# Three heads' keys and queries asked for before the top-k search, in free slots instead of a four-tile ring

## The chip, the cores and the metric

The kernel runs on one core of one Trainium2 chip. A time is device microseconds (us) from the start to the end of one execution. Before the change it is 2321.21 us, the median of three runs (2320.97 to 2325.77). The profile comes from one further execution, which took 2315.68 us.

## The reference

One layer of a decoder block on x of shape 1 x 1024 x 1024: half a SwiGLU feed-forward, a mixer of three branches, half a SwiGLU feed-forward. The mixer, cut to what matters here:

```python
h = rms_norm(x, mix_pre_g)
c_q, c_kv, k_idx_raw, w_idx_raw, u_glu, q_mem, gate_logits = jnp.split(h @ w_in, cuts, axis=-1)
y_a = dsa_attention(...) @ w_dsa_o    # 8 heads of 64; each row attends to its top 256 keys
y_b = conv_module(...)                # causal convolution of 31 taps, ends in w_conv_out
y_m = memory_attention(...) @ w_mem_o # 4 heads of 128 over 256 memory rows
merged = g_a * y_a + g_b * y_b + g_m * y_m      # g_*: sigmoid of the gate logits
return x + rms_norm(merged @ w_out, mix_post_g)

# in dsa_attention, for a block of 128 rows:
score = where(causal, sum over index heads of w * relu(q_idx . k_idx), -1e30)
_, sel = lax.top_k(score, 256)
s = q_lat . ckv[sel]                  # the same number as q . k of the head
p = softmax(where(sel <= position, s, -1e30))
o = (p @ ckv[sel]) @ w_uv             # the same number as p @ v of the head
```

## The kernel before

Everything is kept transposed, in blocks of 128 partitions, and a float32 product is made of three products of a high and a low part (`mm3`, lines 144 to 146). The program runs through feed-forward 1 (to about 700 us), the projections of the mixer, the top-k search with the gate projections beside it (to about 1270 us), the attention with the output projections of the branches as filler (to about 1520 us), the rest of the mixer, and feed-forward 2.

SBUF is 50 equal slots. `blk` takes the slot that has been free longest, `free` gives one back. A ring (`ring(qk=4)`, `rt("qk", ...)`) is a set of slots used in turn: with four tiles it holds K and Q of two heads, and the load of head h + 2 into the tiles of head h has to wait until head h's scores have been computed. The queries, keys and values of all heads lie in DRAM (`qk_spill`, `v_spill`), written by the projections.

`attn` (line 803) goes over two column halves, c = 0 and c = 1 (512 query rows each), and over 8 heads in each, so 16 head steps, which are called h0 to h15 here. A step loads K (256 KB in c = 0, 512 KB in c = 1) and Q (one load of 256 KB and two of 128 KB), four loads in all, issued on GpSimd (POOL), whose loads form the software queue q0. Then come two groups of two row blocks: `weights_of` (line 838) computes the scores (PE, line 851), masks and softmaxes them on VectorE (DVE) and ScalarE (ACT), and `weigh` (line 865) transposes the weights of the group before (line 893), splits them, and multiplies by V (line 881). V is loaded on SyncE (SP), 512 KB a tile, for four heads at a time, by `load_v` (line 781); these loads and all other SP ones are in the hardware queue q1. While a group waits for its softmax, `mix` takes pieces of the generator `outputs` (line 1103): the conv branch through `w_conv_out`, the memory branch through `w_mem_o` with its eight `om` tiles (line 1110), and the first half of the DSA branch. `branch` reads the gates back from `gate_spill` as `sigr` (line 925).

The order of each engine's instructions is not the program's order. A scheduler lays them out once, when the kernel is built, with its own picture of when an operand is there, and the engine then goes through them strictly in turn, and each one waits on its semaphores. A load on POOL that waits for a slot therefore holds up every load behind it on POOL.

In the names of the rows, `K` and `Q` are the tiles of a head, `cbh`/`cbl` the conv branch's parts, `woh`/`wol` those of an output weight, `wor` the raw weight, `st` the staging of the gates.

Of the kernel before, what the change touches and what calls it, by code (L numbers as in the profile page):

```python
# [8 lines left out]
F32 = mybir.dt.float32  # L9
F32R = mybir.dt.float32r  # L10
# [8 lines left out]
P = 128  # L19
# [12 lines left out]
H_A, DH = 8, 64  # L32
# [12 lines left out]
class Kern:  # L45
# [637 lines left out]
    def mem_attn(self):  # L683
        nc, S = self.nc, self.S
        K = self.weight("mk", self.mkv[0].rearrange("p (a b) -> p a b", a=4), [P, 4, NMEM], None, "wr2")
        V = self.weight("mv", self.mkv[1].rearrange("p (a b) -> p a b", a=2), [P, 2, 512], None, "wr2")
# [4 lines left out]
        def scores(h, c):  # L691
# [7 lines left out]
            for t2 in range(2):  # L699
                ps = self.bank("ms").rearrange("p (a b) -> p a b", a=2)  # L700
                for e in range(2):
                    ts = slice((2 * t2 + e) * P, (2 * t2 + e + 1) * P)
                    self.mm3(ps[:, e], (q[:, 0, ts], q[:, 1, ts]), (K[0][:, h], K[1][:, h]), True, True)
                es = slice(2 * t2, 2 * t2 + 2)
# [44 lines left out]
        self.drop("mq", "pm", "pT", "st2")  # L749
        self.free(K, V)  # L750

# [51 lines left out]
    def attn(self):  # L803


        nc, S = self.nc, self.S
        O = S["O"]
        prev = V = None
        self.filled = None
        for c in range(2):  # L810
            if c:
                self.banks(s=[(0, 1)], tp=[2, 3, 4], po=[5], fl=[6, 7])
            for h in range(H_A):
                e = h % 2
                if e == 0:
                    O.append(self.blk("O", [P, 2, 512], F32R))
                K = self.rt("qk", "K", [P, (4 * c + 4) * P], F32R)
                Q = self.rt("qk", "Q", [P, 2, 512], F32R)
                self.load_stack(K, 4 + h // 2, e, 0, (4 * c + 4) * P)
                self.load_stack(Q[:, 0], h // 2, e, c * 512, c * 512 + 512)  # L820
                for r in range(2):
                    nc.gpsimd.dma_start(Q[r * 64:r * 64 + 64, 1].bitcast(F32),
                                      self.qk[h // 2, 1 - r, e * 64:e * 64 + 64, c * 512:c * 512 + 512])
                for g in range(2):
                    i0 = 4 * c + 2 * g
                    p, qk = self.weights_of(Q, K, i0)
                    yield (0.2 * i0 + 0.3) * FILL_A[i0 // 4]
                    if prev:
                        yield from self.weigh(*prev, qk)
                    if h % 4 == 0 and g == 0:  # L830
                        if V:
                            self.free(V)
                        V = self.load_v(h // 4, c)
                    prev = (h, g, i0, p, V, O[-1])
        yield from self.weigh(*prev, None)
        self.free(V)

    def weights_of(self, Q, K, i0):

        nc = self.nc  # L840
        sc = DH ** -0.5
        pair = []
        for i in (i0, i0 + 1):
            n = (i + 1) * P
            ng = 1 if n <= 512 else 2
            n2 = n // ng
            ps = self.bank("s")
            ps = (ps[:, None] if len(ps.shape) == 2 else ps)[:, :ng, :n2]
            for a in range(ng):
                for z in range(2):  # L850
                    mm = nc.tensor.matmul(ps[:, a], Q[:, z, i % 4 * P:(i % 4 + 1) * P], K[:, a * n2:(a + 1) * n2],  # L851
                                          start=z == 0, stop=z == 1)
            p = self.rt("p", "p", [P, n])
            mx = self.sm("amx", 1)
            nc.vector.tensor_tensor_reduce(out=p.rearrange("p (a b) -> p a b", a=ng), in0=ps,
                                           in1=self.S["mask"][i].rearrange("p (a b) -> p a b", a=ng), scale=-sc, scalar=3e38,
                                           op0=OP.add, op1=OP.min, accum_out=mx)
            sm = self.sm("asm", 1)
            nc.scalar.activation(p, p, AF.Exp, bias=mx, scale=-1.0, accum_out=sm)
            nc.vector.reciprocal(sm, sm)  # L860
            nc.vector.tensor_scalar_mul(p, p, sm)
            pair.append(p)
        return pair, mm
# [109 lines left out]
    def build(self):  # L973
        nc, A, S = self.nc, self.A, self.S
# [8 lines left out]
        X, kept, g = {}, [], None  # L983
        for t in range(NT):
            x = self.rt("xt", "x", [P, D])
            nc.sync.dma_start(x, A["x"][t * P:(t + 1) * P])
            if t == 0:
                g = self.bcast("gpre", A["ffn1_pre_g"])
# [85 lines left out]
        for _ in fill:  # L1074
            pass
        self.masks()
        self.topk()
        self.drop("acc", first=True)
        acc = [self.conv(m, u[m]) for m in range(4)]
        self.banks(cn=[0, 1, 2, 3], fl=[4, 5, 6, 7])  # L1080
        cn = self.conv_norm(acc)
        self.ring(qk=4)
        next(cn)
        for e in ends[:-2]:
            self.run(e)
# [31 lines left out]
        self.mix(self.attn(), fill, 1.0)  # L1117
        for _ in fill:
            pass
        self.drop("qk", "p", "pT", "wr", "st", "w")  # L1120
        self.ring(wr=3, w=6, st=3)
        self.free(S["packs"])
        self.banks(two=[(0, 1), (2, 3)], tp=[4, 5, 6, 7], one=[4, 5, 6, 7])
# [6 lines left out]
        g = self.bcast("gpre", A["ffn2_pre_g"])  # L1130
# [5 lines left out]
        for t in range(NT):  # L1136
            c, s = t // 4, slice((t % 4) * P, (t % 4 + 1) * P)
# [348 lines left out]
```

## Time and profile before

| | us |
|---|---|
| median of three runs | 2321.21 |
| lowest, highest | 2320.97, 2325.77 |
| the profiled execution | 2315.68 |
| its span (first to last instruction) | 2313.9 |
| PE busy, of the span | 2226.9 |
| DVE busy, of the span | 1713.8 |

So 1.8 us of the profiled execution lie around its span, and it took 5.53 us less than the median. PE, the matrix engine, is busy 96% of the span; what it is not busy is the waiting of PE, and most of that stands in a few gaps. In the rows below an entry of the timeline is: start in us, duration in us, engine, line, operation, output<-input, the shape, how many such instructions the row takes together, and in brackets the idle time of the engine just before it with what ended it. The granted clock of PE is given as a share of 2.4 GHz: 0.50 is its lower level of 1.2 GHz.

### The profile page before, as it was taken

The numbers are of one execution on the slowest core, as the hardware profiler recorded it, in microseconds if no ns is written. First come the engines' busy times: TensorE is split into PE (matmuls) and PEld (weight loads), VectorE is DVE, ScalarE is ACT, GpSimd is POOL, SyncE is SP. The second block draws the span as 40 slices with busy tenths as digits, with TensorE's granted clock in tenths as the row PEclk, the third lists the DMA queues.
The fourth block names the chain that finished last, engine by engine and source line by source line (L and its number), as shares of the span: only waits on it lengthen the run. The fifth ranks groups of instructions, "written<-read, shape, count | busy, mean of one in ns | idle before, by whom it ended". The sixth has DMA issues, their size and how long they took to land.

```text
span 2313.9 us, 29081 instructions
## 1 busy us (share of the span) xinstructions
PE 2226.9 (96%) x10800; PEld 1370.7 (59%) x10800; DVE 1713.8 (74%) x3000; ACT 1167.5 (50%) x1971; POOL 370.9 (16%) x326
## 2 busy tenths in 40 slices
PE   8799999999999999999999789999899999999998
PEld 5344444444447987888887677778644444444443
DVE  7787777766577699997559677885777777777657
ACT  6644444444435343598995445453564444444423
POOL 2221111111100000120000213330321111111200
PEclk9799999999999999999999999999999999999999
DMA  8111111111224105334332656442422111111112
GB/s 291 44 57 56 59 59 55 55 55 55 86 70 156 51 28 199 129 128 128 101 101 88 187 152 171 132 164 109 146 73 68 57 58 56 55 56 55 45 56 91
DMA packets 163828, 218.87 MB, mean 95 GB/s; under 512 B 26053, under 2 KB 122821, under 8 KB 163687
## 3 DMA queue, kind: packets, MB, share of 16 engines
q1 hardware_dynamic: 141158, 202.23, 26.8%
q0 software_dynamic: 22528, 14.80, 2.6%
q8 instruction: 84, 1.38, 0.2%
q14 instruction: 58, 0.47, 0.1%
HBM read 171.79 MB, written 45.09 MB: 94 GB/s over the span
## 4 chain that ended last, share of the span: by engine, by line
PE 69%; issue 14%; DVE 9%; DMA 3%; ACT 3%; POOL 1%; SPq 0%; POOLq 0%; ACTq 0%; DVEq 0%
PE banks L144 22%; PE banks L146 22%; PE banks L145 21%; PE banks L881 1%; PE banks L851 1%; DVE acc L611 1%; DMA Q<-qk_spill 1%; DMA K<-qk_spill 1%; PE banks L893 1%; DVE xl L283 1%; DVE wts L262 1%; ACT junka L170 1%; DMA qk_spill<-qst 1%; ACT junka L245 1%; PE banks L424 1%
## 5 line engine op out<-in xcount | busy, mean ns | idle before, releaser
L146 PE MATMUL banks<-wds,h 128*128 128x512 f16 x704 | 266.8, 379 | 2.5 <-DVE h L262 2.5
L144 PE MATMUL banks<-xh,wts 128*128 128x512 f16 x704 | 267.7, 380 | 0.9 <-ACT xh L282 0.8
L146 PE MATMUL banks<-xh,wts 128*128 128x512 f16 x704 | 267.3, 380 | 0.0
L145 PE MATMUL banks<-xl,wts 128*128 128x512 f16 x704 | 267.3, 380 | 0.0
L145 PE MATMUL banks<-wds,h 128*128 128x512 f16 x704 | 266.8, 379 | 0.0
L144 PE MATMUL banks<-wds,h 128*128 128x512 f16 x704 | 266.7, 379 | 0.0
L1363 DVE SCALAR_TENSOR_TENSOR y<-banks,scal,y 128x512 f32<-128x512 f32 x288 | 209.4, 748 | 76.0 <-PE banks L146 65.6
L144 PE MATMUL banks<-xh,wh 128*128 128x512 f32 x576 | 226.2, 393 | 0.0
L146 PE MATMUL banks<-xh,wl 128*128 128x512 f32 x576 | 225.9, 393 | 0.0
L145 PE MATMUL banks<-xl,wh 128*128 128x512 f32 x576 | 225.5, 391 | 0.0
L144 PE MATMUL banks<-xh,wt 128*128 128x512 f16 x528 | 202.5, 384 | 4.6 <-DVE t L214 2.8
L146 PE MATMUL banks<-xh,wt 128*128 128x512 f16 x528 | 202.3, 383 | 0.4 <-DVE wt L262 0.4
L145 PE MATMUL banks<-xl,wt 128*128 128x512 f16 x528 | 202.5, 384 | 0.0
L261 ACT ACTIVATE wds<-wd,scal 128x1024 f16<-128x1024 f32 x44 | 47.9, 1139 | 252.7 <-DVE scal L230 230.1
L611 DVE SCALAR_TENSOR_TENSOR acc<-u,convc,acc 128x1023 f32<-128x1023 f32 (+14 forms) x120 | 151.7, 1264 | 0.9
L1311 ACT ACTIVATE sil<-sil,scal 128x512 f32<-128x512 f32 x88 | 63.2, 718 | 142.3 <-DVE sil L1310 142.3
L471 ACT ACTIVATE junka<-sc,tk_neg,tk_sg 128x512 bf16<-128x512 f32 (+1 forms) x124 | 124.1, 1001 | 12.4 <-DVE tk_cand L489 9.4
L1216 POOL TENSOR_TENSOR ws<-wg 128x512 f32<-128x512 f32 x22 | 44.0, 2002 | 499.3 <-DVE wds L262 381.1
L245 ACT ACTIVATE junka<-sil 128x1024 bf16<-128x1024 f32 x44 | 46.5, 1057 | 150.7 <-DVE sil L1327 150.7
L146 PEld LDWEIGHTS banks<-xh,wl 128*128 128x128 f32 x576 | 108.4, 188 | 22.3 <-DVE wl L130 0.2
L145 PEld LDWEIGHTS banks<-xl,wh 128*128 128x128 f32 x576 | 108.4, 188 | 21.5
L144 PEld LDWEIGHTS banks<-xh,wh 128*128 128x128 f32 x576 | 108.4, 188 | 21.3 <-ACT xh L129 0.3
(366 smaller groups left out, 4830.9 us busy)
## 6 DMA issues: line engine op xcount, KB each, us to landing
wg<-in_ffn_w_gu SPq DMA_DIRECT2D x44, 512.0 KB, 3.5
wu<-in_ffn_w_gu SPq DMA_DIRECT2D x44, 512.0 KB, 3.6
wd<-in_ffn_w_down SPq DMA_DIRECT2D x44, 512.0 KB, 4.1
wr<-in_w_in SPq DMA_DIRECT2D x38, 512.0 KB, 3.6
gate_spill<-st SPq DMA_DIRECT2D x24, 512.0 KB, 2.7
x_spill<-xres SPq DMA_DIRECT2D x16, 512.0 KB, 2.6
qk_spill<-qst SPq DMA_DIRECT2D x32, 256.0 KB, 3.3
sigr<-gate_spill SPq DMA_DIRECT2D x16, 512.0 KB, 6.2
```

What stands on the lines that cost most here:

```text
L144: self.first = mm(out, a[0], b[0], start=start, stop=False)
L145: mm(out, a[0], b[1], start=False, stop=False)
L146: return mm(out, a[1], b[0], start=False, stop=stop)
L170: self.nc.scalar.activation(self.junk(x.shape), x, AF.Square, accum_out=ss)
L245: self.nc.scalar.activation(self.junk(x.shape), x, AF.Square, accum_out=ss)
L261: self.nc.scalar.activation(hi, raw, AF.Copy, scale=s)
L262: self.nc.vector.scalar_tensor_tensor(lo, raw, s, hi, op0=OP.mult, op1=OP.subtract)
L471: nc.scalar.activation(self.junk((P, ns[q])), sc[q], AF.Sign, bias=bias[:, z:z + 1], scale=scale, accum_out=cnt[:, z:z + 1])
L611: nc.vector.scalar_tensor_tensor(a[:, s:], u[:, :T - s], self.cc[:, m, j:j + 1], a[:, s:], op0=OP.mult, op1=OP.add)
L1216: V.tensor_add(a[:, 0], lo[:, :, P:], hi[:, :, P:])
L1311: nc.scalar.activation(o, o, AF.Silu, scale=iv)
L1363: V.scalar_tensor_tensor(self.y[t][:, cs], py, iv, self.y[t][:, cs], op0=OP.mult, op1=OP.add)
```

## The change

K and Q no longer have a ring. A new function `load_qk` takes two free slots for each head step and issues its four loads; a counter `nqk` remembers how far it has come. It is called once before the top-k search for h0, h1 and h2, and then at the start of each head step: in c = 0 for all steps up to two ahead, in c = 1 up to one ahead. K and Q of a step go back to the free slots when the scores of its second group have been issued. The loads themselves are the same, 64 in all, as are the products.

```diff
                 e = h % 2
                 if e == 0:
                     O.append(self.blk("O", [P, 2, 512], F32R))
-                K = self.rt("qk", "K", [P, (4 * c + 4) * P], F32R)
-                Q = self.rt("qk", "Q", [P, 2, 512], F32R)
-                self.load_stack(K, 4 + h // 2, e, 0, (4 * c + 4) * P)
-                self.load_stack(Q[:, 0], h // 2, e, c * 512, c * 512 + 512)
-                for r in range(2):
-                    nc.gpsimd.dma_start(Q[r * 64:r * 64 + 64, 1].bitcast(F32),
-                                      self.qk[h // 2, 1 - r, e * 64:e * 64 + 64, c * 512:c * 512 + 512])
+                self.load_qk(8 * c + h + (1 if c else 2))
+                K, Q = self.qks.popleft()
                 for g in range(2):
                     i0 = 4 * c + 2 * g
                     p, qk = self.weights_of(Q, K, i0)
+                    if g == 1:
+                        self.free(K, Q)
...
+    def load_qk(self, last):
+
+        nc = self.nc
+        while self.nqk <= min(last, 2 * H_A - 1):
+            c, h = divmod(self.nqk, H_A)
+            e = h % 2
+            K = self.blk("K", [P, (4 * c + 4) * P], F32R)
+            Q = self.blk("Q", [P, 2, 512], F32R)
+            self.load_stack(K, 4 + h // 2, e, 0, (4 * c + 4) * P)
+            self.load_stack(Q[:, 0], h // 2, e, c * 512, c * 512 + 512)
+            for r in range(2):
+                nc.gpsimd.dma_start(Q[r * 64:r * 64 + 64, 1].bitcast(F32),
+                                    self.qk[h // 2, 1 - r, e * 64:e * 64 + 64, c * 512:c * 512 + 512])
+            self.qks.append((K, Q))
+            self.nqk += 1
...
         self.masks()
+        self.nqk, self.qks = 0, deque()
+        self.load_qk(2)
         self.topk()
...
-        self.ring(qk=4)
...
-        self.drop("qk", "p", "pT", "wr", "st", "w")
+        self.drop("p", "pT", "wr", "st", "w")
```

On POOL, before, the loads of the attention follow the last mask of the top-k search (`mask_9016`) head by head. Here h2 is K_10372 and Q_10373, h3 is K_10470 and Q_10471, h4 is K_10577 and Q_10578:

```order
L440 AFFINE_SELECT mask_9016<-mask_9016 128x128
L794 DMA K_10372<-qk_spill_81 128x1x512
L794 DMA Q_10373<-qk_spill_81 128x1x512
L822 DMA Q_10373<-qk_spill_81 64x512 x2
L794 DMA K_10470<-qk_spill_81 128x1x512
L794 DMA Q_10471<-qk_spill_81 128x1x512
L822 DMA Q_10471<-qk_spill_81 64x512 x2
L794 DMA K_10577<-qk_spill_81 128x1x512
```

h0 and h1 stand ahead of the masks there. At the same place of POOL after the change, h0, h1 and h2 stand ahead of the masks, h3 is K_10283 and Q_10284, h4 is K_10384 and Q_10385, h5 is K_10482 and Q_10483, and h6 is K_10589 and Q_10590 (the waits of each are in brackets; DMASW semaphores count landings of software loads):

```order
L440 AFFINE_SELECT mask_9016<-mask_9016 128x128 [waits DVE_49]
L794 DMA K_10589<-qk_spill_81 128x1x512 [waits DMASW4_49,PE_49]
L794 DMA K_10482<-qk_spill_81 128x1x512 [waits DMASW5_49,PE_49]
L794 DMA Q_10483<-qk_spill_81 128x1x512 [waits DMASW6_49,PE_49]
L794 DMA K_10384<-qk_spill_81 128x1x512 [waits DMAHW3_49,DMAHW5_49,DMAHW1_49,DMAHW7_49,DMASW7_49,DVE_49]
L794 DMA Q_10385<-qk_spill_81 128x1x512 [waits DMAHW3_49,DMAHW1_49,DMAHW7_49,DMASW0_49,DVE_49]
L846 DMA Q_10385<-qk_spill_81 64x512 [waits DMASW1_49]
L794 DMA K_10283<-qk_spill_81 128x1x512 [waits DMASW2_49,PE_49]
L846 DMA Q_10385<-qk_spill_81 64x512 [waits DMASW3_49]
L846 DMA Q_10483<-qk_spill_81 64x512 [waits DMASW4_49]
L794 DMA Q_10284<-qk_spill_81 128x1x512 [waits DMAHW3_49,DMAHW0_49,DMAHW4_49,DMASW5_49,Activation_49]
L846 DMA Q_10284<-qk_spill_81 64x512 [waits DMASW6_49]
```

h2 has moved ahead of the masks, and of the next four heads the scheduler has put h3, the one that PE needs first, behind K of h6, most of h5 and most of h4. On SP, before, five of the eight `om` tiles stand in one row in the middle of the attention:

```order
L134 DMA wor_11764<-in_w_mem_o 128x4x256
L925 DMA sigr_11315<-gate_spill_80 128x1024
L1110 DMA om_11297<-branch_spill_85 128x1024
L1110 DMA om_11296<-branch_spill_85 128x1024
L1110 DMA om_11298<-branch_spill_85 128x1024
L1110 DMA om_11299<-branch_spill_85 128x1024
L1110 DMA om_11300<-branch_spill_85 128x1024
L925 DMA sigr_11407<-gate_spill_80 128x1024
```

At that place of SP after the change (om_11299 to om_11306 are what om_11293 to om_11300 were):

```order
L134 DMA wor_11770<-in_w_mem_o 128x4x256
L1124 DMA om_11300<-branch_spill_85 128x1024
L1124 DMA om_11301<-branch_spill_85 128x1024
L938 DMA sigr_11321<-gate_spill_80 128x1024
L1124 DMA om_11305<-branch_spill_85 128x1024
L1124 DMA om_11304<-branch_spill_85 128x1024
L1124 DMA om_11306<-branch_spill_85 128x1024
L1124 DMA om_11302<-branch_spill_85 128x1024
L1124 DMA om_11303<-branch_spill_85 128x1024
L938 DMA sigr_11413<-gate_spill_80 128x1024
```

The last two of the row are now the fourth and the fifth tile, of which the fourth goes into a slot of K or Q and waits for scores of h9; before, they were the seventh and the eighth.

## Rows read from the trace of the kernel before

**Rows 1.** The page: span, busy time of PE, and the chain that ended last, by line.

```profile
span 2313.9 us, 29081 instructions
PE 2226.9 (96%) x10800; PEld 1370.7 (59%) x10800; DVE 1713.8 (74%) x3000; ACT 1167.5 (50%) x1971; POOL 370.9 (16%) x326
...
PE banks L144 22%; PE banks L146 22%; PE banks L145 21%; PE banks L881 1%; PE banks L851 1%; DVE acc L611 1%; DMA Q<-qk_spill 1%; DMA K<-qk_spill 1%; PE banks L893 1%; DVE xl L283 1%; DVE wts L262 1%; ACT junka L170 1%; DMA qk_spill<-qst 1%
```

**Rows 2.** Waits of PE, 1270 to 1550 us: total, times, longest.

```profile
PE banks L851 <- DMA Q<-qk_spill: 19.9, 7, 10.1
...
PE banks L145 <- DMA om<-branch_spill: 1.5, 2, 1.2
PE banks L144 <- DMA om<-branch_spill: 0.8, 1, 0.8
```

**Rows 3.** Timeline of PE: three of the seven starts that waited for Q.

```profile
1297.63 0.45 PE L851 MATMUL banks<-K,Q 128*128 128x128 f32 x1 [10.13 <-DMA Q<-qk_spill]
...
1318.51 0.30 PE L851 MATMUL banks<-K,Q 128*128 128x128 f32 x1 [1.53 <-DMA Q<-qk_spill]
...
1362.37 1.87 PE L851 MATMUL banks<-K,Q 128*128 128x320 f32 x4 [4.71 <-DMA Q<-qk_spill]
```

**Rows 4.** Windows: length, busy of PE, PEld, DVE, ACT, POOL; clock; DMA share; GB/s.

```profile
1297.60:1301.70 4.10, 3.84 (x14) 3.43 (x15) 1.88 (x9) 1.10 (x4) 0.00 (x0) 0.50 0.31 68
1339.20:1342.60 3.40, 3.36 (x15) 3.39 (x16) 2.51 (x8) 1.07 (x4) 0.00 (x0) 0.50 0.85 205
1362.40:1366.50 4.10, 3.97 (x15) 3.51 (x16) 1.39 (x3) 1.30 (x3) 0.00 (x0) 0.50 0.26 83
1300.00:1400.00 100.00, 86.83 (x467) 71.55 (x467) 74.96 (x190) 50.41 (x112) 22.48 (x32) 0.94 0.57 164
```

**Rows 5.** Timeline of POOL: the last mask, then h2's first loads.

```profile
1263.20 0.68 POOL L440 TENSOR_SCALAR_AFFINE_SELECT mask<-mask 128x128 bf16<-128x128 bf16 x1 [6.43 <-DVE mask L533]
1277.49 0.81 POOL L794 DMA_DIRECT2D K<-qk_spill  x1 [13.61 <-PE banks L851]
1278.30 0.85 POOL L794 DMA_DIRECT2D Q<-qk_spill  x1
```

**Rows 6.** DMA issues, 1045 to 1070 us: count, KB each, median us to landing.

```profile
K<-qk_spill POOLq DMA_DIRECT2D x2, 256.0 KB, 9.7
```

**Rows 7.** DMA issues, 1277 to 1280 us: h2's K and its large Q load.

```profile
K<-qk_spill POOLq DMA_DIRECT2D x1, 256.0 KB, 15.4
Q<-qk_spill POOLq DMA_DIRECT2D x1, 256.0 KB, 19.2
```

**Rows 8.** DMA queues, 1280 to 1285 us: packets, MB, share of 16 engines.

```profile
q1 hardware_dynamic: 1128, 1.41, 94.4%
q0 software_dynamic: 598, 0.14, 17.4%
```

**Rows 9.** DMA queues, 1290 to 1295 us.

```profile
q0 software_dynamic: 770, 0.46, 55.5%
q1 hardware_dynamic: 169, 0.45, 36.5%
```

**Rows 10.** DMA queue q0, 1355 to 1362 us, with little beside it.

```profile
q0 software_dynamic: 1401, 0.81, 50.3%
```

**Rows 11.** Timeline of SP: the first V loads, a gate store, the `om` row.

```profile
1265.95 5.65 SPq L787 DMA_DIRECT2D v<-v_spill  x4
...
1275.33 0.33 SPq L567 DMA_DIRECT2D gate_spill<-st  x1
...
1388.10 3.20 SPq L1110 DMA_DIRECT2D om<-branch_spill  x5
```

**Rows 12.** Timeline of PE: h0's last values and h1's last scores.

```profile
1283.64 0.58 PE L881 MATMUL banks<-pT,v 128*128 128x256 f32 x4
1284.80 0.99 PE L851 MATMUL banks<-K,Q 128*128 128x384 f32 x4
```

**Rows 13.** DMA issues, 1388 to 1392 us: the `om` row.

```profile
om<-branch_spill SPq DMA_DIRECT2D x5, 512.0 KB, 9.7
```

## The prediction

> **What bounds the kernel now.** I read the page first. PE is busy for 2226.9 us of a span of 2313.9, so about 87 us of PE's idling is all that an ordering change can win, and the chain that ended last has the loads of Q and of K among its lines, 1% each [rows 1]. Next come PE's waits in the attention. One name leads them: 19.9 us in seven waits go to Q, the longest 10.1 [rows 2]. The timeline gives the places: 10.13 us before 1297.63, 1.53 before 1318.51, 4.71 before 1362.37, and the other four make up the remaining 3.5 [rows 3]. These are starts of head steps. The third view is the window table: in the 4.1 us behind the first and the last of these gaps, and in 3.4 us from 1339.2 on, the granted clock is 0.50, the lower level of 1.2 GHz, where it averages 0.94 over the whole stretch from 1300 to 1400 [rows 4]. So PE pays for such a gap twice.
>
> Why does h2's Q come so late? POOL issues its last mask at 1263.20, then waits 13.61 us for h0's second scores on PE, and issues h2's K at 1277.49 and its large Q load at 1278.30 [rows 5]. That Q load takes 19.2 us to land and K takes 15.4 [rows 7]: 1278.30 + 19.2 = 1297.5, and PE starts at 1297.63 [rows 3]. Among the early loads, in a calmer stretch, K took 9.7 [rows 6]. The difference is company on the DMA engines: from 1280 to 1285 the hardware queue moved 1.41 MB, the software queue 0.14 [rows 8].
>
> **The change part by part.** I sum against the profiled execution (2315.68, which is 1.8 above its span of 2313.9); the median is 5.53 higher, and I add that at the end.
>
> Removed. h2 is asked for before the top-k search, with some 200 us to land, so its gap of 10.1 goes whole. The later gaps arise because POOL waits for the scores of the step two back before it asks. With a free slot each request goes out one to three steps earlier; a step lasts about 10 us (1297.63 to 1318.51 is two steps [rows 3]), and these gaps are at most 4.71 long, so I let them all go: 19.9 us. The clock: the three windows at 0.50 hold 3.84 + 3.36 + 3.97 = 11.17 us of PE work [rows 4], which at the upper level would take half, so 5.6 more. The whole prize is 25.5. Its uncertain part is the clock: the 1.53 before 1318.51 is followed by no such window in these rows, so what brought the clock down at 1339 may not be Q alone, and 1.7 of the 5.6 may stay.
>
> The three-head request itself costs nothing on POOL: it has the same four loads a step, h2's moved over 200 us ahead, onto an engine that stood idle 13.61 us afterwards [rows 5]. They add 768 KB to the early stretch, about 7 us of the software queue at 0.81 MB in 7 us [rows 10], and nobody waits there until the masks are done. If that cover were gone, POOL's work ahead of the search would be late by some 3 us, four issues of 0.8.
>
> Added, first: head 3. After the change h3's Q stands on POOL behind K of h6, and most of h5 and h4, and h3's K is seventh. POOL goes strictly in turn. I count 2.5 MB of software loads from the first K of h6 through the last piece of h3's Q (K of h6, K and Q of h5, K and Q of h4, K and Q of h3 at 256 KB, and five halves of Q at 128). They start when PE is through the last gate projection, about 1270. In the profile h1's last scores start at 1284.80 [rows 12], and without the gap h2 would start at 1297.63 - 10.13 = 1287.5 and h3 one step later, at about 1297. So 27 us are there for 2.5 MB. At the calm rate of 0.81 MB in 7 us, 116 KB a us [rows 10], it takes 21.5 and h3 is in time. At the rate of the crowded stretch, 0.14 MB in 5 us [rows 8], until 1300, and 116 from there, it is 0.84 MB by 1300, and the other 1.66 take 14.3 more: 1314, a stall of 17, and about 2 for the clock behind it. Half-way rows exist too: from 1290 to 1295 the software queue gets 0.46 MB [rows 9], 92 KB a us, or 27 us in all, which just fits. The hardware queue is lighter than before in this stretch, since half of the eight V loads (2 MB) now need slots that free later. So the bounds are 0 and 19; I take 4.5, next to the row of 0.46 MB, with the clock in it.
>
> The trace has the software queue at 0.14 MB beside 1.41 MB of the hardware queue, and at 0.46 beside 0.45 [rows 8, 9]. The Trainium skill, "DMA: Bandwidth & Descriptors", section "Queues, rings and completion order", says that each DMA engine takes turns between the queues it has work for, a packet at a time. By that rule more software loads asked for at once take turns away from V, which speaks against the change; the rows agree on turns, not on equal bytes. By equal turns the row of 0.46 would hold throughout and the term would stay near 0; by the crowded row it is 19.
>
> Second: V. h0's first values need two V tiles. Before, four V loads went out at 1265.95; after, the second tile of the pair stands on SP behind a gate store that before was issued at 1275.33 [rows 11]. A 512 KB load of SP takes 9.7 in a busy stretch [rows 13], so it is there at 1285.0, and h0's values go on to 1283.64 [rows 12]. That is 0 to 1.4; with the 15.4 us of the slowest K [rows 7] it is 7. I take 1. PE's transposes and h1's scores queue behind that matmul, in turn.
>
> Third: `om`. Before, five loads go out together at 1388.10 and take 9.7 [rows 11, 13], and PE waits 2.3 us for them [rows 2]. After, the fourth tile needs a slot of h9's scores and the fifth is behind it; both were wanted at about 1396, and I put their issue at 1392.6, 4.5 behind the row's start. So the waits lie between -2.3 (gone) and 6 more; I take 2, since fewer loads go together. The chain's row is late then, and the whole memory branch with it, as filler on PE.
>
> Fourth: a fuller stretch. From 1300 to 1400 PE is busy 86.83 and DVE 74.96 [rows 4]. With 13 us less of PE's idling there, DVE is at about 86%, and what PE waits for it grows: nothing to 3; I take 1.
>
> Sum: -25.5 + 4.5 + 1 + 2 + 1 = -17.0. The profiled execution would take 2298.7. On the median, 2321.2 - 17.0 = 2304.2. Behind the attention the order of the engines differs only in places that don't touch PE's waits, and PE bounds there [rows 1], so the saving lasts to the end.
>
> **Rivals.** A, everything hidden: head 3 in time, V in time, `om` at -2.3 to 0. For it: the software queue's calm rate. Against: the eight loads of a stretch that showed 94.4% of the hardware queue [rows 8]. It gives -25.5 + 1 = -24.5, so 2296.7. A figure of the Trainium skill would give it too: in "DMA: Bandwidth & Descriptors", section "Anatomy of one DMA — SWDGE (gpsimd) path", a load takes 2.0 us and its bytes at 436 KB a us, which is 2.6 for K. The trace has 9.7 and 15.4 [rows 6, 7], so the measurement decides, and it leaves A only by the sum above.
>
> B, the first gap comes back in part: h3's Q lands about 6 us later than in my sum, or head 3 and `om` each take their middle (9.5 and 4). For it: POOL's order, h3 behind h6. Against: less in the hardware queue. It gives -17 + 7 = -10, so 2311.
>
> C, nothing measurable: head 3 takes about 14 and the rest of what was added 9. 25.5 - 23 = 2.5 less, 2319.
>
> D, slower: the two queues overrun the DMA engines. The requests of h3 to h6 all stand in the software queue from 1270 on, at 0.14 MB in 5 us [rows 8] until 1300. h3 costs 19 as above, V 7, `om` 6, and the fuller stretch 3: 35 - 25.5 = +9.5, so 2331. It decides from the point where the added waits exceed 25.5, that is when head 3 alone stalls over 15 with V and `om` at their far ends. Against it: V's share of the hardware queue is halved.
>
> E, the change doesn't do what it says: only h2 is ahead, and the later requests wait for slots as before. Then the gap of 10.1 and its 1.9 of clock go, and 7 to 8 of the rest stay: -12, then the added waits of -5: 2314. I count it with B.
>
> **How the numbers follow.** My forecast of 2304 has a chance of 0.45, from 2299 to 2308; A has 0.15; B with E 0.25; C 0.07; D 0.08. A measurement of this kernel can tell about 0.2%, 4.6 us, from no change. Faster by more than that: forecast, A, B, E less 0.02 for B's tail toward C, 0.83. Within it: C and that tail, 0.09. Slower: D, 0.08. The range goes from A's 2296.7 less 2.3 for `om` to a part of C: 2294 to 2317; that leaves out D, most of C and little else.
>
> **What would show it.** The profile after should have no wait of 10 us on Q at about 1287; the row of waits on Q should be near 4 instead of 19.9, all at h3, at about 1297. If it is 0, A holds; if over 10, B or D. K of h6 should be asked for at about 1270 on POOL, before h3's Q. A wait of PE's values (line 881) for V near 1284, and the waits for `om` near 1390, show the second and third. The clock should hold its upper level at 1288 and at 1353. What would make the forecast wrong is a new wait in the attention longer than 6 us, or a loss behind it, where I see no mechanism.

## The result, and the profile after

The changed kernel takes 2308.57 us, the median of three runs (2307.91 to 2309.29), against 2321.21 before: 0.9949 of it, with an interval of 0.9933 to 0.9965. It is faster by 12.6 us, where 17.0 were forecast. A second set of runs gave 2310.01 against 2321.39, 0.9947 [0.9935, 0.9959]. The profiled execution took 2308.57 as well. That is only 7.1 below the profiled execution of before (2315.68), and the experiments come back to this.

In the rows that follow lines 851, 881 and 893 of before are lines 864, 894 and 906. First the page after: span and busy time. PE is busy for as long as before, 0.9 us more; the span is 7.1 shorter [rows 1].

```profile
span 2306.8 us, 29099 instructions
PE 2227.8 (97%) x10800; PEld 1373.0 (60%) x10800; DVE 1716.3 (74%) x3000; ACT 1167.1 (51%) x1971; POOL 378.9 (16%) x326
```

PE's waits after, 1270 to 1550 us (total, times, longest):

```profile
PE banks L894 <- DMA v<-v_spill: 7.1, 1, 7.1
PE banks L145 <- DMA om<-branch_spill: 5.7, 1, 5.7
PE banks L864 <- DVE amx L868: 4.2, 5, 1.2
PE banks L894 <- DVE pT L130: 2.6, 7, 0.7
PE banks L144 <- DMA om<-branch_spill: 0.6, 1, 0.6
```

The row on Q, 19.9 us before [rows 2], is gone altogether. Two others have grown in its place: one wait on V that was not there, and om with 6.3 where it had 2.3. So 19.9 - 7.1 - 4.0 = 8.8 us of waiting are gained. The timeline of PE after gives their places (start, duration, and the idle time in front in brackets), and in the last row h3's first scores, without a wait:

```profile
1293.03 1.08 PE L894 MATMUL banks<-pT,v 128*128 128x256 f32 x4 [7.06 <-DMA v<-v_spill]
...
1306.84 0.33 PE L864 MATMUL banks<-K,Q 128*128 128x128 f32 x2
...
1387.78 0.79 PE L145 MATMUL banks<-om,woh 128*128 128x512 f32 x1 [5.74 <-DMA om<-branch_spill]
```

The windows behind these two gaps, and the stretch from 1300 to 1400 (length, busy of PE, PEld, DVE, ACT, POOL, clock, DMA share, GB/s):

```profile
1293.00:1299.00 6.00, 5.97 (x19) 5.08 (x20) 3.51 (x10) 2.77 (x7) 1.87 (x3) 0.52 1.07 188
1387.80:1394.20 6.40, 5.85 (x15) 4.44 (x16) 0.97 (x3) 0.92 (x2) 0.00 (x0) 0.50 0.96 196
1300.00:1400.00 100.00, 92.01 (x515) 77.00 (x514) 81.23 (x203) 54.17 (x121) 18.59 (x27) 0.95 0.77 192
```

PE again goes at its lower level of 1.2 GHz behind each long gap, for 5.97 + 5.85 = 11.8 us of work (a little of the first window, at 0.52, is at the upper level); before it was 11.2 in three windows [rows 4]. Between these two profiles the clock has given nothing back.

POOL's timeline after shows the order that was read from the program, with h3's K in the seventh place and the last pieces of its Q more than 23 us behind the first load:

```profile
1271.89 1.60 POOL L794 DMA_DIRECT2D K<-qk_spill  x2 [5.85 <-PE banks L146]
1273.48 0.81 POOL L794 DMA_DIRECT2D Q<-qk_spill  x1
1274.26 0.82 POOL L794 DMA_DIRECT2D K<-qk_spill  x1
1275.03 0.83 POOL L794 DMA_DIRECT2D Q<-qk_spill  x1
1275.81 0.60 POOL L846 DMA_DIRECT2D Q<-qk_spill  x1
1276.34 0.89 POOL L794 DMA_DIRECT2D K<-qk_spill  x1
...
1287.88 0.84 POOL L794 DMA_DIRECT2D Q<-qk_spill  x1 [5.05 <-DMA K<-qk_spill]
1292.06 0.53 POOL L846 DMA_DIRECT2D Q<-qk_spill  x1 [3.33 <-DMA Q<-qk_spill]
1295.36 1.03 POOL L846 DMA_DIRECT2D Q<-qk_spill  x2 [2.77 <-DMA K<-qk_spill]
```

SP's timeline after: one V tile at 1270.49, its partner only behind two gate stores at 1277.00, and the five om tiles drawn out over 5.4 us where they took 3.2 before [rows 11].

```profile
1270.49 0.37 SPq L787 DMA_DIRECT2D v<-v_spill  x1
1275.19 1.76 SPq L567 DMA_DIRECT2D gate_spill<-st  x2
1277.00 5.05 SPq L787 DMA_DIRECT2D v<-v_spill  x3
...
1374.01 5.38 SPq L1124 DMA_DIRECT2D om<-branch_spill  x5
```

And the DMA issues after at 1295.3 to 1295.5 us (KB, us to landing): the first of the two halves of Q at 1295.36, h3's last piece.

```profile
Q<-qk_spill POOLq DMA_DIRECT2D x1, 128.0 KB, 9.8
```

It lands at 1295.36 + 9.8 = 1305.2, and h3's scores start at 1306.84. Without the 7 us on V they would have been wanted before it was there. That gave the theory for the experiments: the two new waits are late requests that run into a crowd of software loads, and the wait on V hides that h3's Q is late too. Its rivals: that only the late place of a request makes its wait, that only the crowd does, or that the wait on V hides nothing.

### The profile page after: what moved, and what is told of

Its sections match the earlier page's. It is cut to its first block, busy times and chain, and to the rows that moved or that the text cites. A ratio compares the mean times of both kernels' runs of the same rounds, so it can differ in the third digit from the quotient of the medians.

```text
span 2306.8 us, 29099 instructions
## 1 busy us (share of the span) xinstructions
PE 2227.8 (97%) x10800; PEld 1373.0 (60%) x10800; DVE 1716.3 (74%) x3000; ACT 1167.1 (51%) x1971; POOL 378.9 (16%) x326
## 5 line engine op out<-in xcount | busy, mean ns | idle before, releaser
L471 ACT ACTIVATE junka<-sc,tk_neg,tk_sg 128x512 bf16<-128x512 f32 (+1 forms) x124 | 124.1, 1001 | 12.3 <-DVE tk_cand L489 9.4
```

Of the source, the lines that this page charges most:

```text
L471: nc.scalar.activation(self.junk((P, ns[q])), sc[q], AF.Sign, bias=bias[:, z:z + 1], scale=scale, accum_out=cnt[:, z:z + 1])
```

## The experiments

All were timed in five rounds, except the repeat of the kernel before (one round). Ratios are to the kernel before. Two kernels of different sets are compared by their ratios, since the kernel before came to 2321.4, 2323.6 and 2320.9 in the three sets.

**The changed kernel again** (no edit).

> The changed kernel once more, beside the kernel before, to narrow what it is worth. The medians differ by 12.6 us, the two profiled executions by only 7.1, because the profiled execution of before was 5.5 faster than its median. If the medians are the typical case: 2308 to 2309, 12 to 13 below before. If the profiled executions are: before comes out near 2316, and the difference is 7 to 8.

2310.01, 0.9947 [0.9935, 0.9959]: the medians are the typical case. Its waits are those of the first profile, V 6.5 and om 7.8.

**h2 alone ahead**, on the kernel before:

```diff
-                K = self.rt("qk", "K", [P, (4 * c + 4) * P], F32R)
...
+                K, Q = self.h2 if (c, h) == (0, 2) else self.load_qk(c, h, self.rt, "qk")
...
+                    if (c, h, g) == (0, 2, 1):
+                        self.free(K, Q)
...
         self.masks()
+        self.h2 = self.load_qk(0, 2, self.blk)
```

(`load_qk` here is the seven load lines, with the source of the tiles as an argument.)

> The kernel before with one part of the change: K and Q of h2 stand in two free slots and are asked for ahead of the top-k search; all other heads keep the ring of four tiles. V and om are asked for as in the kernel before. Theory 1 (h2's early request is most of the gain; the later requests pay for what they win): no 10 us gap at 1287; h3 is asked for at about 1277 to 1280 and lands about 1297, just when it is wanted, so 0 to 3 us on Q there, and the four small gaps of 3 to 4 us and the one of 4.7 stay; no wait on V, 2.3 on om. Waits on Q 8 to 11 in all; 2308 to 2311, the same as the whole change within 2. Theory 2 (the free slots bring most of it): h3 takes h2's place in the queue and the gap moves there, 7 to 10 us; 2316 to 2319.

2307.76, 0.9940 [0.9925, 0.9954]: as much as the whole change, though its single executions range from 2302.7 to 2312.6, and the profiled one, 2312.5, is among the slowest. PE's waits in its profile (1270 to 1550 us):

```profile
PE banks L860 <- DMA Q<-qk_spill: 11.0, 8, 3.2
...
PE banks L860 <- DVE part L945: 2.3, 1, 2.3
...
PE banks L145 <- DMA om<-branch_spill: 0.4, 1, 0.4
PE banks L144 <- DMA om<-branch_spill: 0.3, 1, 0.3
```

The gap of 10 is gone, 11.0 in small ones are left, and nothing waits for V. (The wait put down to DVE ends at 1302.12, at h3's first scores, and h3's large Q load lands at 1282.81 + 19.2 = 1302.0, so it may be one more on Q.) So the rest of the change, the free slots and the later heads asked for sooner, takes away these 11.0 us, or 13.3, and puts 7.1 of V and 5.6 more of om in their place. Theory 1 holds, theory 2 falls.

**V's tiles early as well**, on the changed kernel:

```diff
+        self.v0 = self.load_v(0, 0)
...
-                        V = self.load_v(h // 4, c)
+                        V = self.load_v(h // 4, c) if c + h else self.v0
```

> The changed kernel, with the two V tiles of the first four heads asked for ahead of the top-k search too. Nothing else is moved in the program. Theory 1 (PE's wait of 7.1 us on V hid that h3's Q is late: it landed at 1305.2 and was used at 1306.8, 1.6 later): the wait on V goes and one on Q of h3 of 3 to 8 us comes at about 1297; the time falls by 0 to 5, 2304 to 2308. Theory 2 (the waits are independent, h3 is in time since the hardware queue is emptier): no wait above 1 us between 1275 and 1385, the lower clock level there goes as well; the time falls by 9 to 12, 2297 to 2300.

2311.18, 0.9953 [0.9940, 0.9965]: no gain. Some of its waits:

```profile
PE banks L638 <- DVE yt L634: 4.1, 1, 4.1
...
PE banks L864 <- DMA Q<-qk_spill: 2.2, 1, 2.2
```

The wait on V is gone and one of 2.2 on Q has come, but at 1317.9, on h4 and not on h3. The program is laid out otherwise as well: the convolution's norm now costs PE 4.1 just ahead, so that h3 is wanted later; that the two slots taken for 200 us do this is likely but not shown. Neither theory is tested by its time; it was the wrong experiment for the question, and the V slot below takes its place.

**The loads of K and Q in the order of the heads**, on the changed kernel:

```diff
+    def chained(self, ins):
+        self.behind(ins, self.lastq)
+        self.lastq = ins
...
-            self.load_stack(K, 4 + h // 2, e, 0, (4 * c + 4) * P)
+            self.chained(self.load_stack(K, 4 + h // 2, e, 0, (4 * c + 4) * P))
```

(and the same for the three loads of Q)

> The changed kernel, with the loads of K and Q held on POOL in the order of the heads: h3, h4, h5, h6. Theory 1 (V's second tile is late because its transfer shares the DMA engines with the software loads, and because it is asked for at 1277): the wait on V stays at 4 to 8, since just as many software loads stand beside it; h3's Q is there by 1295 instead of 1305; the time is the same within 2 of the changed kernel, 2306 to 2310. Theory 2 (the order of the heads costs the time): the wait on V falls below 2, and the time is 2298 to 2302.

2307.84, 0.9934 [0.9922, 0.9947]: 0.7 to 2.2 below the medians of the changed kernel, with intervals that overlap, so no difference is shown. h3's Q was there at 1299.9 (its last piece is asked for at 1281.38 and takes 18.5), not by 1295, but in time for its scores at 1303.19. Its wait on V was said to stay at 4 to 8, and it fell:

```profile
PE banks L898 <- DMA v<-v_spill: 2.6, 1, 2.6
```

The likely reason is on POOL. With h3 first, the first load waits for PE until 1277.79 (K of h6 went at 1271.89), so the crowd starts 6 us later and V gets through sooner; from 1277.5 to 1282.5 the software queue moved 0.05 MB here and the hardware queue 1.30:

```profile
1277.79 0.84 POOL L794 DMA_DIRECT2D K<-qk_spill  x1 [10.17 <-PE banks L868]
```

**V's second tile in a slot that comes free sooner**, on the changed kernel:

```diff
         for t2 in range(2 * c + 2):
+            if (grp, c, t2) == (0, 0, 1):
+                s = self.free_slots[7]
+                self.free_slots.remove(s)
+                self.free_slots.appendleft(s)
             v = self.blk("v", [P, 8, P], F32R)
```

> The changed kernel, with V's second tile in a slot that comes free some 5 us earlier (at about 1272 instead of 1277), and nothing asked for before the top-k search in addition. Theory 1 (PE's wait of 7 us on V is one of a late request): the wait falls below 2; h3's Q, which landed 1.6 us before its use, then shows as a wait of 2 to 6; 2304 to 2308. Theory 2 (it is one of competition with the software loads): V lands at 1290 or later all the same, the wait stays at 4 to 7, 2308 to 2310.

2304.43, 0.9919 [0.9905, 0.9933]. SP's timeline has both tiles in one row now:

```profile
1270.52 1.72 SPq L791 DMA_DIRECT2D v<-v_spill  x2
```

No wait on V is left, and PE's waits show on Q what it had hidden:

```profile
PE banks L868 <- DMA Q<-qk_spill: 2.8, 2, 1.8
```

Theory 1, also in the time. Two things go with it. PE goes at its lower level behind these waits too, for 5.96 us of work from 1299.8 to 1306.6. And the edit moved more than V's tile: on POOL the last K of the crowd now goes behind h3's loads, and h3's last piece of Q goes out at 1290.07 instead of 1295.36:

```profile
1290.07 0.75 POOL L850 DMA_DIRECT2D Q<-qk_spill  x1 [4.46 <-DMA Q<-qk_spill]
```

It lands 10.4 later, at 1300.5, and PE's second scores of h3 start at 1300.64. So this kernel shows h3 late by less than the changed kernel would without its wait on V: h3 is wanted here at about 1299.39 - 1.82 = 1297.6, and in the changed kernel its Q lands at 1305.2, which gives an estimate of some 7 us.

**K and Q of the first half in a ring of six**, in the order of the heads:

```diff
         while self.nqk <= min(last, 2 * H_A - 1):
             c, h = divmod(self.nqk, H_A)
             e = h % 2
+            if 3 <= self.nqk < H_A:
+                self.free_slots.extendleft((self.own.popleft(), self.own.popleft())[::-1])
...
                     if g == 1:
                         self.free(K, Q)
+                        if not c and h + 3 < H_A:
+                            self.own.extend((self.free_slots.pop(), self.free_slots.pop())[::-1])
```

> The changed kernel, with K and Q of the first column half going round in the six slots of h0 to h2 (three heads deep, so that h3 is asked for when h0's scores are done, h4 when h1's are) and the loads in the order of the heads. At V's transfer only h3's four loads stand beside it, where the changed kernel has twelve. Theory 1 (competition of the software loads makes V late): V's wait below 1.5, and Q of h3 0 to 3 as in the kernel with h2 alone ahead, no other waits on Q until 1340; om as in the changed kernel, 6 to 8; 2302 to 2306. Theory 2 (V's late request does): V's wait stays at 3 to 7; 2306 to 2311.

2312.09, 0.9956 [0.9942, 0.9969]. V's second tile goes out at 1277.60, as late as in the changed kernel, but it lands after 6.7 us, and no wait on V is left. The DMA issues and queues from 1277.5 to 1282.5, first of this kernel:

```profile
q1 hardware_dynamic: 621, 1.66, 95.2%
...
v<-v_spill SPq DMA_DIRECT2D x1, 512.0 KB, 6.7
```

then of the changed kernel:

```profile
q0 software_dynamic: 401, 0.59, 41.9%
q1 hardware_dynamic: 138, 0.52, 28.5%
...
v<-v_spill SPq DMA_DIRECT2D x3, 512.0 KB, 19.6
```

With no byte of the software queue beside it (h3's four loads are asked for at 1280.28 to 1282.43, and none has moved yet) the hardware queue moves 1.66 MB in 5 us, with the crowd 0.52. (The crowd is eight loads out at a time by POOL's row above, not the twelve that the expectation speaks of.) So the late request and the crowd make the wait together, and either cure is enough: the earlier slot, or an empty software queue at the same request. The loss is elsewhere. Its waits on Q:

```profile
PE banks L872 <- DMA Q<-qk_spill: 8.9, 2, 7.9
```

These are h8's, at 1349: the free slots now go to the four V tiles of the second half at 1320 to 1330, beside h8's loads. In the DMA issues from 1317 to 1320 us of this kernel:

```profile
K<-qk_spill POOLq DMA_DIRECT2D x1, 512.0 KB, 29.3
```

The forecast for V was right, and those of no other wait on Q and of the time were wrong: the crowd had only moved.

**om without h9's slots**, on the changed kernel:

```diff
+            s = self.free_slots
+            late = s[3], s[4]
+            for x in late:
+                s.remove(x)
+            s.insert(8, late[1])
+            s.insert(8, late[0])
             om = [tuple(self.blk("om", [P, T], F32R) for _ in range(2)) for _ in range(4)]
```

> The changed kernel, with the two om tiles that took h9's K and Q slots put into slots of the conv branch's parts instead; h9's two slots go to tiles that are asked for later. Theory 1 (PE waits 6 to 8 us for om because these two are asked for late, behind h9's scores, and then share the DMA engines with eight software loads): all five late tiles go out at 1374 to 1376, 3 to 5 earlier; the wait on om falls to 1 to 3, and the lower clock level of some 10 us behind it goes or shrinks; 4 to 9 us less than the changed kernel, 2300 to 2305. Theory 2 (the wait is one of bandwidth: five tiles of 512 KB beside the loads of two heads): the wait stays at 5 to 7, 2307 to 2310.

2300.35, 0.9901 [0.9887, 0.9915], 8 to 10 us below the changed kernel by the times and 11 by the ratios. Its waits on om and the stretch from 1300 to 1400:

```profile
PE banks L145 <- DMA om<-branch_spill: 0.8, 1, 0.8
...
PE banks L144 <- DMA om<-branch_spill: 0.5, 1, 0.5
```

```profile
1300.00:1400.00 100.00, 96.75 (x555) 80.61 (x554) 85.14 (x211) 57.07 (x127) 21.46 (x29) 1.00 0.79 196
```

The wait falls by 5.0 and the clock stays at its upper level through the whole stretch, worth another 2.9 (half of 5.85). The five tiles go out within 3.2 us again, and the middle time to landing is 8.6 instead of 12.0. Theory 1, with one thing open: the next loads on POOL now start at 1376.41, behind all five, where in the changed kernel they start at 1376.93, ahead of the last two (1378.59 and 1379.08), so the late request and the crowd are cured together here.

**Three edits together**: order of the heads, V slot, om slots.

> Three edits together on the changed kernel: loads of K and Q in the order of the heads, V's second tile in the earlier slot, om without h9's slots. If each wait is one of a late request, none over 2.5 us is left in the attention: 10 to 14 us below the changed kernel, 2295 to 2299. If the DMA engines are what is short, waits of 3 to 7 come back on Q, V or om, and it is 2301 to 2306.

2295.38, 0.9880 [0.9866, 0.9894]. No wait on V is left, 0.7 on om and 1.2 on Q, but a new one has come at 1343:

```profile
PE banks L872 <- DVE pT L130: 4.1, 1, 4.1
```

DVE is late there because a gate tile (`sigr`) is, as DVE's timeline shows:

```profile
1340.88 0.69 DVE L957 TENSOR_TENSOR part<-banks,sigr 128x512 f32<-128x512 f32 x1 [3.20 <-DMA sigr<-gate_spill]
```

The time is at the lower end of what was expected; the claim that no wait over 2.5 is left was wrong.

**The V slot and the om slots, POOL's order left to the scheduler**:

> The version of 2295.4 without its fixed order of the loads: V's second tile in the earlier slot and om without h9's slots, POOL's loads as in the changed kernel (h3 behind h4 to h6). Theory 1 (h3's place behind three later heads costs PE's waits on Q once V no longer hides them): waits on Q of 2 to 3 us at about 1297, as with the V slot alone (2.8), 2297 to 2300. Theory 2 (V and om are all of it): waits on Q below 1, 2294 to 2296.

2293.60, 0.9884 [0.9864, 0.9904]. Waits in its profile:

```profile
PE banks L868 <- DMA Q<-qk_spill: 2.2, 2, 1.5
```

The window behind them (length, busy of PE, PEld, DVE, ACT, POOL, clock, DMA share, GB/s):

```profile
1300.70:1304.10 3.40, 3.18 (x12) 3.02 (x13) 2.04 (x7) 0.49 (x2) 1.67 (x2) 0.50 0.90 215
```

The waits on Q are those of theory 1, the time that of theory 2. The expectation was wrong about POOL: its order is the one of the V slot alone, with h3 ahead of the last K of the crowd (h3's last piece goes out at 1291.27). So h3's place costs 2.2 us of waits here and half of 3.18, 1.6, by the clock. Putting it first gains nothing that shows, since the two ratios, 0.9880 and 0.9884, lie well inside each other's interval; whether the wait of 4.1 at 1343 comes from the fixed order was not tested. This version beats both kernels, by some 27 us and 15 us.

**The kernel before again** (no edit).

> The kernel before once more, for a second profile: the first one's execution (2315.7) is below every timed run of it (2318.1 and more), so some 5 to 6 us of its usual time aren't in the rows read from it. If they lie in the attention: the wait on Q at 1287 is 12 to 15 us instead of 10.1, or the small gaps are longer, and the change's sum of waits goes up by that. If they lie ahead of 700 us or spread over the phases: the waits on Q are the same 19 to 21, and the starts of the phases are late by 3 to 6 us.

2321.27 in eight runs; its profiled execution took 2319.27. Its wait on Q is longer than in the first profile of before:

```profile
PE banks L851 <- DMA Q<-qk_spill: 21.1, 10, 10.9
```

From PE's 6,001st matrix instruction (at about 1280) to its 8,001st (about 1700) it takes 429.3 us, the first profile 426.4, the two profiles of the change 417.5 and 417.0. So 2.9 of the 3.6 us between the two profiled executions of before lie in the attention, and the change is worth 9 to 12 us there. The waits on Q explain 1.2 of it. The clock is the larger part; these are the stretches of the second profile at the lower level:

```profile
1299.00:1304.40 5.40, 5.15 (x20) 4.55 (x20) 2.01 (x9) 1.19 (x5) 0.00 (x0) 0.50 0.10 30
1321.50:1328.30 6.80, 5.54 (x20) 4.98 (x21) 3.57 (x12) 2.08 (x6) 0.00 (x0) 0.50 0.44 111
1355.60:1359.10 3.50, 3.50 (x14) 3.09 (x13) 2.25 (x8) 1.79 (x6) 0.00 (x0) 0.51 0.64 143
1400.00:1403.40 3.40, 3.04 (x6) 1.66 (x6) 1.04 (x2) 0.00 (x0) 0.00 (x0) 0.50 1.06 311
```

They hold 17.2 us of PE's work where the first profile had 11.2 [rows 4]; half of the difference is 3.0. So the same program, with waits on Q of nearly the same size, pays 5.6 us for the clock in one execution and 8.6 in another. In the second profile of the change it is 10.7 us of work, so 5.3. Single executions of the kernel before range from 2315.5 to 2327.5; why the clock falls behind a small gap in one of them and not in another was not found out.

## Why the prediction came out as it did

The sign, the range and the mechanism of the main step were right: 2308.6 lies in 2294 to 2317, between the forecast and rival B, and 0.6 above the forecast's own band of 2299 to 2308. The sum was too high, by more than the medians show: against its own profiled execution it said 17.0, and the two profiled executions differ by 7.1. By its own sign the forecast was wrong as well, since a new wait of more than 6 us has come, on V; and its sign for A, no wait on Q, misled, since the row was empty only because PE stood for V. The terms one by one:

- **Waits on Q, 19.9.** Right; the row is gone.
- **The clock, 5.6 back.** Wrong for this pair of profiles. I removed three gaps with their clock, and of what was added only head 3 was priced with it; the gaps on V and om were priced without. Each of them, 6 or 7 us long, brought the lower level again, and 11.8 us of work at 1.2 GHz after stand against 11.2 before. Kernel om without h9's slots shows the other side: one gap less, and the level stays up. Between the second profiles, 17.2 before and 10.7 after, 3.3 us did come back.
- **V, 1.** Mis-sized: 7.1, which is my far end. I took 9.7 us for the tile's landing from a stretch without such a crowd; the issue at 1277.00 was 1.7 later than I put it, and from there to PE's start at 1293.03 it is 16.0. I had priced the crowd of software loads for h3's Q, but in the 1 us for V, which stood beside the same loads, it had no part.
- **om, 2.** Mis-sized: 6.3 - 2.3 = 4.0, within the bounds. The row of five is drawn out to 1379.4 (1374.01 + 5.38), since its last two tiles wait for h9's scores.
- **Head 3, 4.5.** 0 in the row, but only since PE stood 7.1 us for V. With the V slot it is 2.8 and, with the clock, some 5.8, but there h3's loads also go out sooner; in the order that I priced it would have been some 7 by the estimate above, without the clock. h3's Q landed at 1305.2, in the middle of what I had bounded: the 2.5 MB took 33.3 us from 1271.89, 75 KB a us, less than the 92 that I had taken as just fitting.
- **A fuller stretch, 1.** Not seen: the waits on DVE in the attention are 7.3 after and 7.8 before (pT and p rose from 2.1 to 3.1, and 1.5 on wol went), although DVE's share of the stretch rose from 75% to 81%.

Against the sum of 17.0, V took 6.1 more, om 2.0 more and the clock 5.9 more (5.6 not given back, 0.3 more lost), head 3 took 4.5 less and the fuller stretch 1 less: 17.0 - 6.1 - 2.0 - 5.9 + 4.5 + 1 = 8.5. PE's time from its 6,001st to its 8,001st instruction fell by 426.4 - 417.5 = 8.9. The whole executions differ by only 7.1, since PE comes to the 6,001st at 1278.0 before and at 1279.7 after, and 1.2 of that is there by 445 us, in feed-forward 1, which the change does not touch. For the second pair the same terms give 21.1 - 6.5 - 4.9 + 3.3 = 13.0, against 429.3 - 417.0 = 12.3. So what the change is worth depends on how much of the lower clock level an execution of the kernel before happens to have. The medians show 12.6 since the first profile of before was a quick execution of its kernel; so part of the agreement with the forecast is luck.

Of the rivals, A (everything hidden) was no result of this change, but with V and om in better slots the change goes there and a little beyond (2293.6 against 2296.7). D named the right mechanism, the two queues on the same DMA engines, with a price too high. Its threshold was added up wrongly too: with V at 7, om at 6 and the fuller stretch at 3, the added waits pass 25.5 from 9.5 us on head 3, not from 15. E, that only h2's request matters, I had priced at 2314 and counted under B; h2 alone gives 2307.8, since it leaves V and om alone, so the price of its added waits was what was wrong.

The sentence of the Trainium skill on turns ("DMA: Bandwidth & Descriptors", "Queues, rings and completion order") spoke against the change, and the trace agrees with it in kind: with both queues at work they moved nearly the same in 5 us, 0.59 MB of the software queue and 0.52 of the hardware queue, which alone had moved 1.66. I had named it for V and priced it for Q alone. Its direction for V was the one that counted.

## What to carry to other kernels

When requests are moved ahead, ask what else is in flight when they now run, and price each transfer that PE needs next, not only the ones that are moved. Of two loads that are late at the same time only the later one shows, so the other comes up when the first is cured; slots should go first to what is wanted first. A gap that is added can cost its clock as well as its length, as the one that is removed did: every gap of 4 us and more in these attentions came with a stretch at the lower level. And an edit of slots lets the scheduler lay out the loads anew, so the order of issue of each version has to be read before its time is explained.

## What the runs showed of the hardware that was not expected

A K of 512 KB on the software queue took 29.3 us to land in the ring of six, where 256 KB had taken 9.7 in a calm stretch [rows 6]; and 512 KB on the hardware queue took 16.0, to PE's start, beside eight software loads and 6.7 where the software queue had moved nothing yet.

The two queues together moved less beside the crowd, but not by one amount. Hardware loads alone moved 1.66 MB in 5 us, 332 GB/s, at a share of 95.2%. In the two windows behind the gaps of the changed kernel the share is 1.07 and 0.96, and 188 and 196 GB/s are moved. From 1277.5 to 1282.5 the changed kernel moved 0.59 + 0.52 = 1.11 MB, 222 GB/s, with the engines at 41.9 + 28.5 = 70.4%, and with the V slot, beside eight software loads as well, it was 1.50 MB:

```profile
q0 software_dynamic: 591, 0.76, 55.6%
q1 hardware_dynamic: 207, 0.74, 41.2%
```

That is a tenth less than without the crowd, at a share of 96.8%. So a crowd of software loads takes about half of what is moved, and the sum is lower by a tenth to more than two fifths; what sets its size was not found out.
